# Streaming encoder step: three weight buffers in an empty operand region, and other pacing of operand building and of a reload

## The chip, the cores and the metric

The kernel runs on one core of one Trainium2 chip. A core has five engines with queues of their own: TensorE (matmul; PE in the rows, its weight loads PEld), VectorE (DVE), ScalarE (ACT), GpSimd (POOL) and SyncE (SP), which here issues the DMAs. Each engine runs its instructions in a fixed order, and an instruction that waits holds all behind it on its engine. The metric is the device time of one execution in microseconds (us), and lower is better. The kernel before took 1099.64 us (median of 3 runs, 1098.98 to 1100.81).

## The reference, cut to what matters

One step of a two-layer encoder over 1024 prompt rows and 64 rows of a running stream, 1088 in all. Layer 0 is a gated short convolution, layer 1 latent attention; everything that the edit touches lies in layer 0:

```python
def short_conv_mixer(h, conv_prev, w_in, conv_w, w_out):
    T = h.shape[1]
    b_gate, c_gate, xv, z = jnp.split(h @ w_in, 4, axis=-1)
    u = c_gate * xv
    up = jnp.concatenate([conv_prev.astype(u.dtype), u], axis=1)
    conv = up[:, 0:T] * conv_w[0]
    for k in range(1, CONV_WIDTH):
        conv = conv + up[:, k:k + T] * conv_w[k]
    y = (jax.nn.silu(z) * b_gate * conv) @ w_out
    return y, up[:, -(CONV_WIDTH - 1):]
```

`h` is the RMS-normed input (1024 channels), `w_in` is 1024 x 4096, all in float32. In layer 1 follow projections, attention with 16 heads and an output product, and at the end a last norm.

## The kernel before

**Precision.** Each float32 operand is split into a high part (`whi`, `bhi`, `t1h`: a cast on ScalarE) and a low part (`wlo`, `blo`, `t1l`: original less high part, on GpSimd or VectorE), and a product is three matmuls: high x high, high x low, low x high. `load_w` (L273 to L297) does it for a block of weights of 128 x 1024: a DMA into `wraw` (three buffers), the cast (L288), the subtraction (L292). `whi` and `wlo` have two buffers each.

**Layer 0.** The 1088 columns are two halves of 544 (`sc` = 0, 1), each two pieces of 272 (`c`). The output channels are eight tiles of 128 (`ct`), with four parts each (b, c, x, z).

- *Plain tiles*, ct = 0, 1, 2 of the first half: `conv_mm` makes 24 matmuls for each part and piece, so 48 for a block of weights. For ct = 1 and 2 one block is loaded ahead (`ahead`, L868 to L874). PSUM banks 0 to 4 take the results in turn.
- *Pairs*: for the other tiles two parts are computed together by a Strassen-like scheme: seven products (`p1`, `p5`, `p3` of the pair before, `p6`, `p4` of the pair before, `p2`, `p7`) of twelve matmuls each, on sums of weights and sums of inputs. `prep` makes the weight sums: `unit` splits a whole block (ScalarE and GpSimd), the pieces `t1`, `t2`, `t4` come from VectorE and ScalarE (L674 to L687). There are 10 pairs of the first half, then 16 of the second.
- *Operands of the pairs*: `build(sc, k)`, k = 0 to 3, makes the sums of inputs. `build(0, k)` runs beside the plain tiles (VectorE and GpSimd), `build(1, k)` beside the pairs of the first half (all on GpSimd). `squares(k)` sums the squares for the second half's norm: a ScalarE square into PSUM bank 7, a VectorE addition, in turn.
- *Gates*: `conv_evac` and `conv_tail` take results out of PSUM; part z goes VectorE (L532), ScalarE (L533), GpSimd (L534), VectorE (L536).
- *Reload*: the gated result of the first half goes to memory (`y_scratch`) and is read back by `reload_y` (L506 to L514) for the output product, once the last pair of the first half is done.

**What sets the order.** `jobs` is a list of generators; `side()` advances the first by a step, after each product (seven in a pair) and twice after each piece of a plain tile. `issue_after` on the last low subtraction keeps a job's instructions behind it. A scheduler turns the program into one order for each engine. The empty operand region is `R1`: its first 8704 columns hold the inputs of the plain tiles (`HS`, `LS`), its last 2048 the last block of ct = 0, and the rest is unused until `build(1, ...)`.

Of the kernel before, what the change touches and what calls it, by code (L numbers as in the profile page):

```python
# [25 lines left out]
KD = D // P  # L26
# [15 lines left out]
def r32(ap):  # L42
    return ap.bitcast(F32)
# [166 lines left out]
def kernel(ctx, tc, xT, small, w1, w2, w3, w3r, wpair, wqr, wv, wkT, w4,  # L210
# [13 lines left out]
    def nm(s):  # L224
        cnt[0] += 1
        return f"{s}_{cnt[0]}"
# [9 lines left out]
    def gps(tag="g", size=1):  # L236
        (b0, b1), k = turns[tag]
        turns[tag][1] = (k + size) % (b1 - b0)
        return PS[:, b0 + k:b0 + k + size, :].rearrange("p b n -> p (b n)")
# [27 lines left out]
    def ordered(ins):  # L267
        if keep_order[0]:
            tc.keep_in_program_order(ins)
# [4 lines left out]
    def load_w(src, n, view=None, into=None, lo_engine=None, cuts=None, shared=False):  # L274
        raw = wp[0].tile([P, WN[0]], F32, tag="wraw", name=nm("wraw"), bufs=3)
        if into is None:
            hi = wp[0].tile([P, WN[0]], F32R, tag="whi", name=nm("whi"), bufs=WN[1])
            lo = wp[0].tile([P, WN[0]], F32R, tag="wlo", name=nm("wlo"), bufs=WN[1])
        else:
            hi, lo = into  # L280
        if cuts:
            def part(a, b):
                ordered(A.copy(out=hi[:, a:b], in_=raw[:, a:b]))
                ordered((lo_engine or G).tensor_sub(lo[:, a:b], raw[:, a:b], r32(hi[:, a:b])))
            return hi, lo, lambda a, b: SP.dma_start(out=raw[:, a:b], in_=src[:, a:b]), part
        dst = raw[:, :n] if view is None else view(raw[:, :n])
        SP.dma_start(out=dst, in_=src)
        ins = A.copy(out=hi[:, :n], in_=raw[:, :n])  # L288
        hi_on[0] = ins.ins
        ordered(ins)  # L290
        m = n // 2 if shared else n
        ins = (lo_engine or G).tensor_sub(lo[:, :m], raw[:, :m], r32(hi[:, :m]))  # L292
        lo_on[0] = ins.ins
        ordered(ins)
        if shared:
            V.tensor_sub(lo[:, m:n], raw[:, m:n], r32(hi[:, m:n]))
        return hi, lo  # L297
# [77 lines left out]
    SC = 2 * NS  # L375
    REG = 14 * 4 * NS
    pX = tc.alloc_tile_pool(name="pX", bufs=1, side="right")
    R1 = pX.tile([P, REG], F32R, name="R1")
# [30 lines left out]
    def yh(k, c0, c1):  # L409
        return YHV[:, k, c0:c1]  # L410
# [15 lines left out]
    def staged(k):  # L426

        o = (2 * (k % 2) + k // 4) * SC
        return (STG, ST2)[k % 4 // 2][:, o:o + SC]
# [35 lines left out]

    def conv_mm(c, W, lag=0, mid=None):

        cs = slice(c * NS, (c + 1) * NS)
        wh, wl = W
        ps = gps()[:, :NS]  # L470
# [35 lines left out]
    def reload_y():  # L506

        for k in range(KD):
            y = STG[:, (k % 4) * SC:(k % 4 + 1) * SC]
            SP.dma_start(out=y, in_=y_d[k][:, :SC])  # L510
            yield
            A.copy(out=yh(k, 0, SC), in_=y)
            G.tensor_sub(yl(k, 0, SC), y, r32(yh(k, 0, SC)))  # L513
            yield  # L514

    def conv_state(ct, sc, u):
        if sc == 0:
# [69 lines left out]
    def build_first(k):  # L587
        yield from build(0, k)
        yield
        for kk in (k, k + 4):  # L590
            SP.dma_start(out=staged(kk), in_=xT[kk][:, SC:])
        yield

    def squares(k):

        for kk in (k, k + 4):
            for c in range(2):
                q, t = staged(kk)[:, c * NS:(c + 1) * NS], PS[:, 7, :NS]
                s = rb[:, SC + c * NS:SC + (c + 1) * NS]
                if kk == 0:  # L600
                    A.activation(out=s, in_=q, func=AF.Square)
                else:
                    A.activation(out=t, in_=q, func=AF.Square)
                    V.tensor_add(s, s, t)
                if k == 3:
                    yield
            if k < 3:
                yield

    jobs = []  # L610
# [182 lines left out]
    PARTS = [1, 2, 3, 0]  # L793
    STD = 3
    pairs = [f for sc, cts in ((0, range(STD, KD)), (1, range(KD))) for ct in cts for f in conv_pairs(ct, sc)]
    split_psum(g=(0, 6), q=(6, 8))
    ahead = []
    for ct in range(STD):
        if ct == 0:
            u, z = new_u(ct, 0), new_z()  # L800
            W = {}
            keep_order[0] = True
            *w, dma, part = load_w(w1[ct][PARTS[0]], 1024, lo_engine=V, cuts=True)
            W[PARTS[0]] = w
            dma(0, 256)
            x_dma(0, 0)
            dma(256, 1024)
            for k in range(1, KD):
                x_dma(0, k)
            part(0, 256)  # L810
            x_split(0, 0)
            part(256, 640)
            x_split(0, 1)
            part(640, 1024)
            for k in range(2, KD):
                x_split(0, k)
            *w, dma, part = load_w(w1[ct][PARTS[1]], 1024, lo_engine=V, cuts=True)
            W[PARTS[1]] = w
            dma(0, 1024)
            part(0, 512)  # L820
            part(512, 1024)
            pe_order[0] = True
            held = {c: [] for c in range(2)}

            def first(c, pi, lag=0, mid=None):
                held[c].append(conv_mm(c, W[PARTS[pi]], lag, mid))

            def evac(c, *pis):
                for pi in pis:
                    conv_evac(0, u, z, PARTS[pi], c, held[c][pi])  # L830

            first(0, 0, 3)
            for i, part in enumerate((3, 0)):
                W[part] = load_w(w1[ct][part], 1024, lo_engine=V, into=[p1.tile([P, 1024], F32R, tag=x, name=nm(x), bufs=1) for x in ("bhi", "blo")] if part else
                                 [R1[:, REG - n:REG - n + 1024] for n in (2048, 1024)])
                for k in range(2 * i, 2 * i + 2):
                    x_square(0, k)
            first(0, 1, 6)
            for k in range(KD):
                x_dma(1, k)  # L840
            for k in range(4, KD):
                x_square(0, k)
            first(0, 2, KD)
            first(0, 3, KD)
            for k in range(KD):
                x_split(1, k)
            end = finish_x(0)
            first(1, 0)
            first(1, 1, 0, end)
            evac(0, 0, 1)  # L850
            for k in range(4):
                x_square(1, k)
            first(1, 2)
            for k in range(4, KD):
                x_square(1, k)
            evac(0, 2, 3)
            first(1, 3)
            end = finish_x(1)

            def rest(u=u):  # L860
                end()
                evac(1, 0, 1, 2, 3)
                conv_state(0, 0, u)

            keep_order[0] = False
            split_psum(g=(0, 5), q=(7, 8))
            turns["g"][1] = 2
            jobs.extend([build_first(0), build_first(1), squares(0), build_first(2), squares(1), build_first(3), squares(2)])  # L868
        else:
            for pi, part in enumerate(PARTS):  # L870
                W = ahead.pop() if ahead else load_w(w1[ct][part], 1024)
                if pi < 3 or ct + 1 < STD:
                    ahead.append(load_w(w1[ct + (pi == 3)][PARTS[(pi + 1) % 4]], 1024))
                    paced["lo"] = lo_on[0]  # L874
                for c in range(2):
                    ps = conv_mm(c, W, (KD, 0)[c])
                    if ct == 1 and pi == c == 0:
                        rest()
                    if pi == c == 0:
                        u, z = new_u(ct, 0), new_z()  # L880
                    conv_evac(ct, u, z, part, c, ps)
                    side(2)
                if ct == STD - 1:
                    with tc.issue_after(lo_on[0]), tc.issue_after(hi_on[0]):
                        step(0, (0, 1, 1, 4)[pi])
        if ct:
            conv_state(ct, 0, u)
# [6 lines left out]
    def second_half():  # L894
        todo = {}

        def at(t, f):
            todo.setdefault(t, []).append(f)

        def factors():  # L900
            todo[9] = [rstd([rb[:, SC:]], rb[:, SC:], D, SC)]

        at(3, factors)
        for k in range(4):
            steps = build(1, k)
            for t in (0, 5, 6, 12):
                at(11 + 12 * k + t, lambda steps=steps: next(steps, None))
        for t in range(64):
            for f in todo.get(t, []):
                f()  # L910
            yield

    jobs.extend([squares(3), second_half()])
    step(1)

    pairs[2 * (KD - STD)].whole = True
# [19 lines left out]
    for dt in range(KD):  # L936
# [5 lines left out]
        for c, (c0, c1) in enumerate(CHK):  # L942
            n = c1 - c0
# [203 lines left out]
    for c, (c0, c1) in enumerate(CHK):  # L1147
        n = c1 - c0
# [675 lines left out]
    for dt in range(KD):  # L1824
# [9 lines left out]
        for c0, c1 in GRP[0]:  # L1834
            n = c1 - c0
# [125 lines left out]
```

## Time and profile before

| | us |
|---|---|
| median of 3 runs | 1099.64 |
| the profiled execution | 1099.2 |
| its span | 1097.4 |
| TensorE busy | 1048.0 (95%) |
| VectorE busy | 754.0 (69%) |
| ScalarE busy | 638.3 (58%) |
| GpSimd busy | 532.1 (48%) |

In the profile the busy times say how full an engine is over the whole span; a stage is read from its own rows. ct = 0 ends at about 36 us, the plain tiles of ct = 1 and 2 at 93.9, the pairs at about 383; output product, projections and attention follow. In a row of an engine in order of time stand its start, its duration, line, operation, output <- input, count, and in brackets the idle time before it with what released it.

### The profile page before, as it was taken

To read this page: it belongs to the slowest core of one execution; us is meant where nothing else is said; L and a number is where in the kernel's file an instruction comes from. 1 tells how busy PE (TensorE), PEld (TensorE's weight loads), DVE (VectorE), ACT (ScalarE), POOL (GpSimd) and SP (SyncE) were. 2 spreads that over 40 slices of the span, in tenths; PEclk is the share of its full clock that TensorE was granted. 3 is DMA by queue.
4 is the path that set the end of the run, shared out by engine and by line. 5 is a ranking of instruction groups with operands and counts; after the bars stand their busy time and mean duration, and the time that the engine had idled before them with its cause. 6 is when DMAs were issued, how large, how long until landed. Compare 5 with 4: busy or idle time off the path is not lost.

```text
span 1097.4 us, 19670 instructions
## 1 busy us (share of the span) xinstructions
PE 1048.0 (95%) x7123; PEld 1003.3 (91%) x7123; DVE 754.0 (69%) x1523; ACT 638.3 (58%) x1388; POOL 532.1 (48%) x446
## 2 busy tenths in 40 slices
PE   9989998989999999999899999999999999989994
PEld 8979998989999999999798999899999999879983
DVE  6888666756666445555996432788888888896456
ACT  5446676666666533345522334877787778785352
POOL 0475698886576622113452322445555545563243
PEclk9999999999999999999998999999999999999997
DMA  7244232442323244422142114433422331334224
GB/s 236 69 129 147 88 124 92 134 153 84 116 79 114 82 151 140 133 99 80 53 139 104 34 50 115 104 80 87 109 57 66 88 90 47 103 120 150 89 85 155
DMA packets 58145, 114.55 MB, mean 104 GB/s; under 512 B 8080, under 2 KB 32400, under 8 KB 58048
## 3 DMA queue, kind: packets, MB, share of 16 engines
q1 hardware_dynamic: 57840, 112.97, 33.7%
q8 instruction: 56, 0.92, 0.4%
q14 instruction: 41, 0.34, 0.1%
q10 hardware_dynamic: 144, 0.26, 0.1%
q0 software_dynamic: 64, 0.07, 0.0%
HBM read 79.27 MB, written 16.31 MB: 87 GB/s over the span
## 4 chain that ended last, share of the span: by engine, by line
PE 69%; DVE 10%; POOL 5%; issue 5%; DMA 4%; ACT 4%; SPq 1%; POOLq 0%; DVEq 0%; ACTq 0%
PE PS L301 48%; PE PS L1487 16%; PE PS L1526 5%; DMA QB<-stg 3%; POOL wlo L1765 1%; DMA wraw<-in_w 1%; POOL wlo L292 1%; DVE PS L488 1%; ACT PH L1539 1%; DVE OL L1011 1%; ACT stg L1603 1%; POOL R L565 1%; SPq L1613 1%; DVE PL L1543 0%; POOL R L513 0%
## 5 line engine op out<-in xcount | busy, mean ns | idle before, releaser
L301 PE MATMUL PS<-R,whi 128*128 128x272 f32 (+2 forms) x1662 | 370.4, 313 | 15.4 <-ACT whi L288 4.4
L301 PEld LDWEIGHTS PS<-R,whi 128*128 128x128 f32 x1662 | 276.6, 191 | 20.1 <-ACT whi L288 5.1
L301 PE MATMUL PS<-R,wlo 128*128 128x272 f32 (+2 forms) x888 | 265.9, 311 | 1.2 <-POOL wlo L292 1.2
L292 POOL TENSOR_TENSOR wlo<-wraw,whi 128x1024 fp32r<-128x1024 f32 x36 | 88.7, 2465 | 185.5 <-ACT whi L288 179.6
L301 PEld LDWEIGHTS PS<-R,wlo 128*128 128x128 f32 x888 | 164.1, 190 | 2.4 <-POOL wlo L292 1.9
L1487 PE MATMUL PS<-KB,QB 96*128 96x512 f32 (+11 forms) x576 | 125.2, 355 | 1.1 <-DVE SZ L1031 0.6
L1521 POOL TENSOR_SCALAR Pt<-Pt,st 128x640 f32<-128x640 f32 (+3 forms) x64 | 61.4, 961 | 86.4 <-DVE st L1517 85.9
L1487 PEld LDWEIGHTS PS<-KB,QB 96*128 96x128 f32 (+1 forms) x576 | 94.4, 190 | 9.4 <-DVE PL L1543 1.1
L1504 DVE TENSOR_REDUCE st<-PS 128x1 f32<-128x1024 f32 (+7 forms) x128 | 94.7, 748 | 10.9 <-PE PS L1487 10.2
L1543 DVE TENSOR_TENSOR PL<-PS,PH 128x512 fp32r<-128x512 f32 (+3 forms) x192 | 98.7, 547 | 3.1 <-ACT PH L1539 1.8
L1539 ACT CAST PH<-PS 128x512 fp32r<-128x512 f32 (+3 forms) x192 | 85.4, 497 | 14.7 <-PE PS L1526 13.5
L1487 PE MATMUL PS<-PH,VB 128*128 128x256 f32 x320 | 76.5, 279 | 0.0
L637 POOL TENSOR_TENSOR wlo<-wraw,whi 128x1024 fp32r<-128x1024 f32 x26 | 62.5, 2404 | 27.1 <-ACT whi L636 24.2
L1487 PE MATMUL PS<-PL,VB 128*128 128x256 f32 x320 | 75.3, 282 | 0.2 <-DVE PL L1543 0.2
L1513 ACT ACTIVATE Pt<-PS,st 128x640 f32<-128x640 f32 (+3 forms) x64 | 62.1, 970 | 5.7 <-DVE st L1517 2.6
L301 PE MATMUL PS<-R,bhi 128*128 128x272 f32 x320 | 61.1, 289 | 2.6 <-DVE z L763 1.0
L1487 PEld LDWEIGHTS PS<-PH,VB 128*128 128x128 f32 x320 | 60.8, 190 | 1.3 <-DVE PL L1543 0.8
L1487 PEld LDWEIGHTS PS<-PL,VB 128*128 128x128 f32 x320 | 61.1, 191 | 0.7 <-DVE PL L1543 0.4
L288 ACT CAST whi<-wraw 128x1024 fp32r<-128x1024 f32 (+1 forms) x37 | 38.2, 1033 | 38.3 <-PE PS L301 20.6
L1526 PE MATMUL PS<-ident,Pt 128*128 128x128 f32 x416 | 55.4, 274 | 0.2 <-ACT Pt L1513 0.2
L301 PEld LDWEIGHTS PS<-R,bhi 128*128 128x128 f32 x320 | 49.6, 188 | 3.7 <-DVE z L763 1.2
L1568 POOL TENSOR_TENSOR SZ<-SZ,ot 64x256 f32<-64x256 f32 x64 | 47.0, 746 | 11.7 <-DVE ot L1563 9.4
(438 smaller groups left out, 2623.0 us busy)
## 6 DMA issues: line engine op xcount, KB each, us to landing
wraw<-in_w SPq DMA_DIRECT2D x83, 512.0 KB, 3.6
KB<-stg SPq DMA_DIRECT2D x32, 256.0 KB, 3.8
QB<-stg SPq DMA_DIRECT2D x32, 256.0 KB, 4.7
braw<-in_w SPq DMA_DIRECT2D x13, 512.0 KB, 4.4
QB<-qr_scratch SPq DMA_DIRECT2D x32, 128.0 KB, 3.1
x<-x_scratch SPq DMA_DIRECT2D x8, 416.0 KB, 3.2
xr<-in_xT SPq DMA_DIRECT2D x16, 192.0 KB, 2.4
x_scratch<-xr SPq DMA_DIRECT2D x16, 192.0 KB, 1.9
```

The costliest lines, as they stand in the source:

```text
L288: ins = A.copy(out=hi[:, :n], in_=raw[:, :n])
L292: ins = (lo_engine or G).tensor_sub(lo[:, :m], raw[:, :m], r32(hi[:, :m]))
L301: ins = PE.matmul(ps, lhsT, rhs, start=start, stop=stop, skip_group_check=more)
L637: ins = eng.tensor_sub(lo, src, r32(hi))
L1487: pin(PE.matmul(ps, lhsT, rhs, start=start, stop=stop))
L1504: pin(V.tensor_reduce(out=st[:, 0:1], in_=TL["S", h, i], axis=AX.XY, op=ALU.max, negate=True))
L1513: pin(A.activation(out=Pt, in_=TL.pop(("S", h, i)), func=AF.Exp, bias=st[:, 0:1], accum_out=st[:, 1:2]))
L1521: pin(G.tensor_scalar(Pt, Pt, st[:, 2:3], 1.0, op0=ALU.mult, op1=ALU.mult))
L1526: pin(PE.transpose(out=tp[:, j * P:(j + 1) * P], in_=TL["P", h, i][:, (j0 + j) * P:(j0 + j + 1) * P], identity=ident))
L1539: pin(A.copy(out=hi, in_=src))
L1543: pin(V.tensor_sub(lo, src, r32(hi)))
L1568: pin(G.tensor_mul(sz, sz, TL.pop(("ot", h, pr))[rows]))
```

## The change

Line numbers after it are higher by 1 from L512 and by 3 at the end.

- The blocks of ct = 1 and 2 no longer go to `whi` and `wlo` but to three buffers of 2 x 1024 columns in `R1`, from column 8704, and up to three are loaded ahead. The third buffer (columns 12800 to 14848) overlaps the last block of ct = 0, and it takes the first load. `wraw` keeps its three buffers.
- `squares(2)` goes from the jobs of the plain tiles to those of the pairs, ahead of `squares(3)`, so `second_half` begins two steps later.
- In `second_half` the second and third step of a `build(1, k)` come at 6 and 7 instead of 5 and 6 steps after its first.
- `reload_y` waits six steps instead of one after each of its eight blocks.

```diff
@@ reload_y
             A.copy(out=yh(k, 0, SC), in_=y)
             G.tensor_sub(yl(k, 0, SC), y, r32(yh(k, 0, SC)))
-            yield
+            for _ in range(6):
+                yield
@@ plain tiles
-    ahead = []
+    ahead, todo = [], [(t, p) for t in range(1, STD) for p in PARTS]
@@
-            jobs.extend([build_first(0), build_first(1), squares(0), build_first(2), squares(1), build_first(3), squares(2)])
+            jobs.extend([build_first(0), build_first(1), squares(0), build_first(2), squares(1), build_first(3)])
         else:
             for pi, part in enumerate(PARTS):
-                W = ahead.pop() if ahead else load_w(w1[ct][part], 1024)
-                if pi < 3 or ct + 1 < STD:
-                    ahead.append(load_w(w1[ct + (pi == 3)][PARTS[(pi + 1) % 4]], 1024))
+                while len(ahead) < 3 and todo:
+                    n, (t, p) = len(todo) % 3, todo.pop(0)
+                    o = 2 * KD * SC + n * 2048
+                    ahead.append(load_w(w1[t][p], 1024, into=[R1[:, o + i:o + i + 1024] for i in (0, 1024)]))
                     paced["lo"] = lo_on[0]
+                W = ahead.pop(0)
@@ second_half
-            for t in (0, 5, 6, 12):
+            for t in (0, 6, 7, 12):
@@
-    jobs.extend([squares(3), second_half()])
+    jobs.extend([squares(2), squares(3), second_half()])
```

Three places of the engines' orders. GpSimd at the entry to the pairs, before (`wlo_860` and `wlo_934` are the last two plain blocks, `blo_1001`, `wlo_1084` and `wlo_1110` belong to pairs 0 and 1, L565 builds operands, L534 is the gate):

```order
L292 TENSOR_TENSOR wlo_860<-wraw_858,whi_859 128x1024
L565 TENSOR_TENSOR R_104<-ST_107,R_104 128x2x272 x2
L292 TENSOR_TENSOR wlo_934<-wraw_932,whi_933 128x1024
L637 TENSOR_TENSOR blo_1001<-braw_928,bhi_1000 128x1024
L534 TENSOR_TENSOR z_819<-z_819,acc_100 128x272
L637 TENSOR_TENSOR wlo_1084<-wraw_929,whi_1083 128x1024
L534 TENSOR_TENSOR z_819<-z_819,acc_100 128x272
L637 TENSOR_TENSOR wlo_1110<-wraw_1088,whi_1109 128x1024
```

And now (`R_98<-wraw_850` is the last plain block):

```order
L292 TENSOR_TENSOR R_98<-wraw_850,R_98 128x1024
L566 TENSOR_TENSOR R_104<-ST_107,R_104 128x2x272
L638 TENSOR_TENSOR blo_977<-braw_918,bhi_976 128x1024
L638 TENSOR_TENSOR wlo_1060<-wraw_919,whi_1059 128x1024
L638 TENSOR_TENSOR wlo_1086<-wraw_1064,whi_1085 128x1024
L566 TENSOR_TENSOR R_104<-ST_107,R_104 128x2x272
L535 TENSOR_TENSOR z_811<-z_811,acc_100 128x272 x2
```

The last plain block is done one place earlier, and three blocks of the pairs stand ahead of the last operand piece and of both gates.

VectorE at the same place, before (L532 is the gate of the second last plain block, for its two pieces; L675 to L687 and L637 make the pairs' pieces):

```order
L565 TENSOR_TENSOR R_104<-ST_107,R_104 128x2x272
L530 TENSOR_TENSOR u_817<-PS,u_817 128x272
L604 TENSOR_TENSOR acc_100<-acc_100,PS 128x272
L488 SCALAR_TENSOR_TENSOR PS<-u_817,sm,PS 128x272
L675 TENSOR_TENSOR wraw_929<-wraw_929,PS 128x512
L532 TENSOR_TENSOR z_819<-PS,acc_100 128x272
L488 SCALAR_TENSOR_TENSOR PS<-u_817,sm,PS 128x272
L676 TENSOR_TENSOR PS<-PS,braw_928 128x512
L637 TENSOR_TENSOR t1l_1070<-PS,t1h_1069 128x512
L532 TENSOR_TENSOR z_819<-PS,acc_100 128x272
```

And now, up to the same second gate (L580 to L583 make the last operand's sums):

```order
L566 TENSOR_TENSOR R_104<-ST_107,R_104 128x2x272
L638 TENSOR_TENSOR t1l_1046<-PS,t1h_1045 128x512
L680 TENSOR_TENSOR PS<-wraw_919,PS 128x512
L533 TENSOR_TENSOR z_811<-PS,acc_100 128x272
L638 TENSOR_TENSOR t2l_1051<-PS,t2h_1050 128x512
L688 TENSOR_TENSOR PS<-braw_918,PS 128x512
L676 TENSOR_TENSOR wraw_1065<-wraw_1065,PS 128x512
L677 TENSOR_TENSOR PS<-PS,wraw_1064 128x512
L533 TENSOR_TENSOR z_811<-PS,acc_100 128x272
```

More of the pairs' pieces stand ahead of the second gate, and the two L676/L677 of pair 0, which stood behind L565, are now among the sums ahead of L566.

GpSimd in the reload, before, from one `t4l` to the next (L513 is a reload block, L504 the second half's result):

```order
L637 TENSOR_TENSOR t4l_2564<-t_250_2561,t4h_2563 128x512
L637 TENSOR_TENSOR wlo_2725<-wraw_2622,whi_2724 128x1024
L513 TENSOR_TENSOR R_104<-STG,R_104 128x544 x2
L637 TENSOR_TENSOR wlo_2783<-wraw_2760,whi_2782 128x1024
L513 TENSOR_TENSOR R_104<-STG,R_104 128x544
L504 TENSOR_TENSOR R_104<-y_2826,R_104 128x272
L513 TENSOR_TENSOR YLB<-STG,R_104 128x544
L637 TENSOR_TENSOR t4l_2704<-t_267_2701,t4h_2703 128x512
```

And now:

```order
L638 TENSOR_TENSOR t4l_2682<-t_251_2679,t4h_2681 128x512
L638 TENSOR_TENSOR blo_2852<-wraw_2738,bhi_2851 128x1024
L513 TENSOR_TENSOR R_104<-STG,R_104 128x544
L504 TENSOR_TENSOR R_104<-y_2847,R_104 128x272
L638 TENSOR_TENSOR wlo_2905<-braw_2886,whi_2904 128x1024
L638 TENSOR_TENSOR t4l_2824<-t_270_2821,t4h_2823 128x512
```

One reload block stands between two `t4l` instead of four. In SyncE's queue the load of the fifth reload block stood ahead of a pair's second block of weights and now stands behind it.

## Rows read from the trace of the kernel before

**Rows 1.** Chain of waits, plain tiles: start us, us, what.
```profile
45.16 2.56 DVE R L576
...
89.79 4.84 DMA wraw<-in_w
```

**Rows 2.** TensorE's waits, 60 to 94 us: line, for whom, total us, times, longest.
```profile
PE PS L301 <- ACT whi L288: 4.4, 3, 2.8
PE PS L301 <- POOL wlo L292: 1.2, 3, 0.5
```

**Rows 3.** TensorE in order of time, plain tiles and entry to the pairs.
```profile
36.28 2.25 PE L301 MATMUL PS<-R,whi 128*128 128x272 f32 x16
...
49.49 2.16 PE L301 MATMUL PS<-R,whi 128*128 128x272 f32 x16
...
55.48 2.16 PE L301 MATMUL PS<-R,whi 128*128 128x272 f32 x16
...
64.43 3.48 PE L301 MATMUL PS<-R,whi 128*128 128x272 f32 x16 [2.81 <-ACT whi L288]
...
93.91 0.41 PE L301 MATMUL PS<-R,bhi 128*128 128x272 f32 x2
...
98.55 0.52 PE L301 MATMUL PS<-R,t2h 128*128 128x272 f32 x2 [1.47 <-ACT p L707]
```

**Rows 4.** VectorE in order of time, 37 to 93 us.
```profile
37.94 0.16 DVE L331 TENSOR_TENSOR rst<-rsy 128x3 f32<-128x3 f32 x1
...
45.07 2.65 DVE L576 TENSOR_TENSOR R<-STG,R 128x272 fp32r<-128x272 f32 x1
...
82.89 0.44 DVE L579 TENSOR_TENSOR ST<-ST 128x272 f32<-128x272 f32 x1 [2.16 <-POOL R L565]
...
92.45 0.43 DVE L532 TENSOR_TENSOR z<-PS,acc 128x272 f32<-128x272 f32 x1
```

**Rows 5.** GpSimd in order of time, plain tiles and reload.
```profile
45.03 2.40 POOL L292 TENSOR_TENSOR wlo<-wraw,whi 128x1024 fp32r<-128x1024 f32 x1 [1.45 <-ACT whi L288]
...
61.22 2.46 POOL L534 TENSOR_TENSOR z<-z,acc 128x272 f32<-128x272 f32 x1 [2.24 <-ACT z L533]
...
81.50 1.36 POOL L565 TENSOR_TENSOR R<-ST,R 128x544 fp32r<-128x544 f32 x1
...
232.36 2.68 POOL L513 TENSOR_TENSOR R<-STG,R 128x544 fp32r<-128x544 f32 x2
```

**Rows 6.** ScalarE in order of time, plain tiles and a build.
```profile
34.59 0.47 ACT L486 ACTIVATE PS<-u,sm 128x272 f32<-128x272 f32 x1
...
86.20 1.03 ACT L288 CAST whi<-wraw 128x1024 fp32r<-128x1024 f32 x1
...
166.25 0.42 ACT L575 CAST R<-ST 128x272 fp32r<-128x272 f32 x1 [4.25 <-POOL ST L573]
```

**Rows 7.** TensorE in order of time, builds of the second half and reload.
```profile
170.87 0.52 PE L301 MATMUL PS<-R,whi 128*128 128x272 f32 x2 [1.87 <-ACT p L707]
...
172.93 0.52 PE L301 MATMUL PS<-R,whi 128*128 128x272 f32 x2 [0.28 <-DVE z L771]
...
176.88 0.52 PE L301 MATMUL PS<-R,whi 128*128 128x272 f32 x2 [0.68 <-DVE u L763]
...
227.27 0.51 PE L301 MATMUL PS<-R,whi 128*128 128x272 f32 x2 [0.62 <-ACT p L707]
...
244.78 0.52 PE L301 MATMUL PS<-R,whi 128*128 128x272 f32 x2 [1.78 <-DVE u L763]
...
246.04 0.66 PE L301 MATMUL PS<-R,whi 128*128 128x272 f32 x2
...
249.42 0.42 PE L301 MATMUL PS<-R,t4h 128*128 128x272 f32 x2
```

**Rows 8.** VectorE in order of time, reload.
```profile
242.06 0.69 DVE L684 TENSOR_TENSOR t<-wraw,PS 128x512 f32<-128x512 f32 x1 [2.38 <-POOL t4l L637]
```

**Rows 9.** Busy time of GpSimd in a stretch: us, busy us, count, TensorE's clock, DMA share, GB/s.
```profile
230.00:242.00 12.00, 12.00 (x9) 1.00 0.38 126
```

## The prediction

> **What bounds the kernel now.** Read in this order: the busy rows of the page, the waits of TensorE in the plain stretch, the chain of waits there, then each engine's instructions in order of time. TensorE is busy 95% of the span, so only its idle stretches and its slow stretches can give time back. In the plain tiles of ct = 1 and 2 it waits 4.4 us for `whi` casts and 1.2 us for `wlo` subtractions [rows 2]; after the longest wait, 2.81 us, sixteen matmuls take 3.48 us instead of 2.16, another 1.3 us at the lower of the two clock levels [rows 3]. That is 6.9 us, and three weight buffers aim at it.
>
> The reader should see the other half in the chain of waits: from 45.16 us to the DMA that ends at 94.6 it holds pieces of VectorE, ScalarE, GpSimd and DMA and none of TensorE [rows 1]. TensorE's waits there are slack beside a longer chain: operand building, gates and squares, in fixed order on VectorE, ScalarE and GpSimd. So the first question is when that chain lets the first pair start, not when the weights are ready.
>
> Two more stretches belong to the edit. In the builds of the second half TensorE waits 1.87, 0.28 and 0.68 us, right after ScalarE sat 4.25 us in front of a cast that needs GpSimd's product [rows 6, 7]. In the reload it waits 0.62 and 1.78 us [rows 7], the latter behind VectorE, which waited 2.38 us for a late GpSimd subtraction [rows 8]; the stretch after it is slow: five triples of matmuls from 246.04 to 249.42 take 3.38 us [rows 7], where the normal pace is 48 in 5.99 us (49.49 to 55.48 [rows 3]), 0.374 for a triple and 1.50 for a product of twelve, so 1.5 us are lost.
>
> **The weights' buffers.** The order shows the eight casts at the same places in ScalarE's row, each now one load ahead. Casts 4 to 8 wait for TensorE to have left the buffer three tiles back, which it has. The first load goes to the third buffer, which overlaps the last weights of ct = 0; its cast stands behind ScalarE's gate product that ends at 35.06 [rows 6], when TensorE is past most of them, so the cast (1.03 us [rows 6]) ends at 36.1 and TensorE, free at 36.28 [rows 3], does not wait. The subtraction behind it (2.40 us [rows 5]) runs to 38.6, when the sixteen `hi` matmuls are just done. It costs something else: it lies beside the root chain of 128x3 products that begins at 37.94 [rows 4]. The nearest row of two such instructions is a VectorE subtraction of 272 columns with both inputs in SBUF, which took 2.65 us beside a `wlo` subtraction begun at 45.03 and ended when that ended, against 0.44 alone [rows 4, 5]. So the price is between 0 and 0.6 (37.94 to 38.6); I take 0.6, since the row shows full blocking.
>
> The Trainium skill (SBUF — State Buffer, Who interferes with whom) says that VectorE instructions with two SBUF inputs and GpSimd instructions that read SBUF exclude each other whatever their size, and that the one issued first holds the port to its end. By that rule the term is 0.6, without it 0; the 2.65 us row agrees, while the product of 2.46 us at 61.22 [rows 5] shows GpSimd losing to several VectorE instructions in a row.
>
> From there a plain tile takes 5.99 us. Eight tiles end near 87.2, with some 1.1 us of waiting left at tile 7, whose cast stands late in ScalarE's order; before, the last ended at 93.9. TensorE gains 6.7 us here, if anything can follow.
>
> **The entry to the pairs.** The first product of pair 0 needs PSUM bank 0, which the second gate evacuation of tile 7 frees (L532 before, L533 now). Before, that ran from 92.45 to 92.88, 1.0 us ahead of the product at 93.91 [rows 3, 4], so it cost nothing. Now TensorE arrives at 87.2 and it decides. The order rows show what VectorE does first: the four sums of the last operand, eight pieces of the pairs' operands, two conv products. And GpSimd has `blo` and two `wlo` subtractions, 2.4 us each, ahead of the last operand and of the gates, where it had one of the plain weights and then gaps.
>
> Up to 82.86 both orders are alike: GpSimd's subtraction of 81.50 ends and VectorE's L579 (now L580) starts at 82.89 [rows 4, 5]. Before, GpSimd had nothing ready then. Now `blo_977` is ready (its cast no longer waits behind squares), so it runs from 82.86 to 85.26, and by the 2.65 us row the VectorE sum then ends at 85.55 instead of 83.25: 2.3 us. L676, L531, L581 and L677 (0.69 us for a wide one [rows 8], 0.44 for a narrow one [rows 4], each overlapping the next by 0.1) bring VectorE to 87.45; the cast of the next `wlo` starts when L676 is done, 1.03 us [rows 6], so that GpSimd starts at 87.4. One of L582 and L583 meets it and waits: 1.9 us. L566 meets the third one: 1.55. Some 0.6 of these lies beside casts that the chain awaits anyway. Unblocked, the same list ends at 92.8, no sooner than before; with the three blocks at 98.05, with the 0.6 of above at 98.65. A fourth meeting (L582 as well) would make it 100.5, one less 97.4.
>
> So the first product starts at 98.65. Two products later (1.50 us each) is 101.65, and after some 11 us of idling I add one slow stretch, 1.3 us as at 64.43 [rows 3] (bounds 0 and 2.5). The third product, at 98.55 before [rows 3], stands at 102.95: **4.4 us lost** (bounds: 0.8 gained with no block, 6.5 lost with four). The casts and subtractions hoisted there are then done, so I expect no more waits in pairs 0 and 1.
>
> **Squares moved.** squares(2), four ScalarE and four VectorE instructions, leaves the crowded stretch and goes beside pairs 0 and 1, where TensorE has 21 us of work. The norm's matmuls stand two products later too, so I cost it at nothing; without that cover it is some 0.9 us for each of four (a narrow VectorE row of 0.44 and a narrow ScalarE row of 0.42 [rows 4, 6]).
>
> **Steps of the second half.** The cast that ScalarE stood 4.25 us in front of comes one product later (1.5 us), and in the new order two GpSimd subtractions with their casts pass between the product and that cast, so ScalarE no longer holds the gates behind it. I take all of 1.87 + 0.28 + 0.68 = **2.8 us gained** (bounds: 1.0 lost, if the later end of the builds makes pair 10 wait for as much as the 0.62 of [rows 7] or a little more, and 2.8). The end of the builds comes two steps later and should have room: pair 10 needs the last operand in its second product.
>
> **Reload.** Up to the `t4l` subtraction that ended at 242.06 GpSimd was busy for 12.0 of 12 us [rows 9], where a pair's seven products take TensorE 10.5: it is the slower of the two there. The order has four reload subtractions between that `t4l` and the one before it, 1.34 us each (two took 2.68 [rows 5]). In the new order one stands there, which takes 4.0 off: 8.0, well under 10.5. The 1.78 and the slow stretch of 1.5 go; the reload's DMA now stands behind the weights' in SP's queue, so the 0.62 goes too: **3.9 us gained** (bounds 1.8 and 4.4). The rest of the reload spreads over seven pairs, 1.4 us of GpSimd in each, which brings GpSimd to 9.4 at most where it had 8.0. After the pairs every engine's order is the same as before.
>
> **Sum.** 1099.2 (the profiled execution, span 1097.4 and 1.8 around it) + 4.4 - 2.8 - 3.9 = 1096.9. The median of the runs is 0.4 above that execution, so **1097.3**.
>
> **Rivals.** *The blocking does not add up* (17%): VectorE gets in between GpSimd's subtractions, as at 61.22. The first product then starts at 93.45, the third at 97.75, 0.8 gained; with the other two terms 7.5: 1092.1. For it: the one row of 2.46; against it: the 2.65.
> *The waits were the bound* (4%): everything that TensorE waited is recovered, the third product at 90.2, 8.3 gained: 1084.6. Against it stands the chain without TensorE.
> *Slower* (24%): the same blocking, once more. Four meetings put the first product at 100.5, and the clock stays low for 2 us of loss: 6.5 lost; and the builds gain nothing because GpSimd, late there, now only holds up a later cast. With 3.3 of the reload 3.2 us are lost: 1102.8. With the builds' gain the point from which it decides is a first product after 101.0.
> *It does not do what it says* is the forecast's own first half: the buffers remove the waits and no time.
>
> **How the numbers follow.** Forecast 55%, its own range 1094 to 1101. A change of 0.2%, 2.2 us, is about what a measurement of this kernel can tell from none. Of the forecast's 55 parts 26 lie more than 2.2 below 1099.64, 25 within, 4 above; the first two rivals are faster (21), of the slower one 20 parts lie above, 4 within. So faster 0.47, same 0.29, slower 0.24. The range runs from 1091 to 1103: it holds most of the first rival and most of the slower one.
>
> **What would show it.** Right: no wait of TensorE for `whi` in the plain tiles; the first product of pair 0 waiting some 11 us for VectorE's gate (98 to 101 us), with VectorE sums of over 2 us beside GpSimd subtractions from 82.9 on; the first reduced clock after that and none near 246; no ScalarE wait of 4 us for the builds; GpSimd with gaps in the reload. Wrong: a first product before 94 us, VectorE's sums at 0.44 throughout, or new waits in pairs 10 to 17.

## The result: 12 us slower, and the profile after

The changed kernel takes 1111.63 us (median of 4 runs), the kernel before 1099.80: a ratio of 1.0111 [1.0077, 1.0145]. The forecast was 1097.3, so the sign is wrong too. The profiled execution after takes 1111.65 us, its span is 1109.9.

TensorE in order of time, from ct = 0 to the entry of the pairs (answers [rows 2, 3]):

```profile
30.27 1.21 PE L301 MATMUL PS<-ident,rsy 128*128 128x128 f32 x6 [2.69 <-DVE rsy L333]
...
44.68 0.93 PE L301 MATMUL PS<-ident,rsy 128*128 128x128 f32 x6 [0.74 <-DVE rsy L333]
...
91.48 4.79 PE L301 MATMUL PS<-R 128*128 128x272 f32 x24 [2.53 <-DVE u L531]
...
103.65 0.79 PE L301 MATMUL PS<-R,bhi 128*128 128x272 f32 x2 [7.38 <-DVE z L533]
...
109.22 0.43 PE L301 MATMUL PS<-R,t2h 128*128 128x272 f32 x2
```

The waits for `whi` in the plain tiles are gone but for 0.39 us at 78.95 us and 0.46 us for a subtraction at 81.68, as forecast (some 1.1 left). In their place stand waits for VectorE: 2.69 us already in ct = 0, where there was none, 2.53 in the last plain tile, 7.38 in front of the first product of pair 0. The third product (109.22) is 10.7 us later than in [rows 3], not 4.4. After the first of these waits the granted clock was 0.59 from 30 to 34 us: from 30.27 to the sums of the second root (40.08) pass 9.81 us, where the same stretch takes 8.41 in run 3 below.

VectorE (answers [rows 4]), then GpSimd (answers [rows 5]), then ScalarE (answers [rows 6]):

```profile
24.11 2.32 DVE L331 TENSOR_TENSOR rst<-rsy 128x3 f32<-128x3 f32 x1
26.47 2.29 DVE L332 SCALAR_TENSOR_TENSOR rst<-rst,rsv 128x3 f32<-128x3 f32 x1
...
41.04 1.62 DVE L328 TENSOR_SCALAR rst<-rsv 128x3 int32<-128x3 int32 x1
...
87.89 2.59 DVE L580 TENSOR_TENSOR ST<-ST 128x272 f32<-128x272 f32 x1 [3.06 <-POOL R L566]
...
92.30 2.60 DVE L582 TENSOR_TENSOR ST<-ST 128x272 f32<-128x272 f32 x1
...
95.23 2.19 DVE L583 TENSOR_TENSOR ST<-ST 128x272 f32<-128x272 f32 x1
...
103.07 0.43 DVE L533 TENSOR_TENSOR z<-PS,acc 128x272 f32<-128x272 f32 x1
```

```profile
24.01 4.73 POOL L292 TENSOR_TENSOR R<-wraw,R 128x1024 fp32r<-128x1024 f32 x2 [22.70 <-ACT R L288]
...
40.25 2.38 POOL L292 TENSOR_TENSOR R<-wraw,R 128x1024 fp32r<-128x1024 f32 x1 [1.34 <-PE PS L301]
...
86.49 1.36 POOL L566 TENSOR_TENSOR R<-ST,R 128x544 fp32r<-128x544 f32 x1
87.81 2.37 POOL L638 TENSOR_TENSOR blo<-braw,bhi 128x1024 fp32r<-128x1024 f32 x1
92.23 4.89 POOL L638 TENSOR_TENSOR wlo<-wraw,whi 128x1024 fp32r<-128x1024 f32 x2 [2.06 <-ACT whi L637]
```

```profile
22.89 1.99 ACT L288 CAST R<-wraw 128x1024 fp32r<-128x1024 f32 x2
...
211.27 0.65 ACT L565 CAST R<-ST 128x544 fp32r<-128x544 f32 x1 [4.18 <-POOL ST L582]
```

Read the first two fences side by side. Each long VectorE instruction begins while a GpSimd subtraction runs and ends when that ends or up to 0.3 us later; the same 128x3 operation takes 0.16 us in [rows 4]. At 24 us two subtractions in a row catch two root instructions in a row. They can run then because the casts of the second and third load find empty buffers at 22.89 us. Before, the first two casts of the plain blocks stood so, and the first subtraction behind them so:

```profile
25.19 1.05 ACT L288 CAST whi<-wraw 128x1024 fp32r<-128x1024 f32 x1 [2.64 <-issue]
...
28.82 1.05 ACT L288 CAST whi<-wraw 128x1024 fp32r<-128x1024 f32 x1
```

```profile
26.33 2.39 POOL L292 TENSOR_TENSOR wlo<-wraw,whi 128x1024 fp32r<-128x1024 f32 x1 [25.01 <-ACT whi L288]
```

The first idled 2.64 us at the same place of ScalarE's order; the row names no releaser, by the program it is TensorE leaving `whi`. The second stood behind four other ScalarE instructions (L346, L444 and two L447), which it now precedes. At 88 us it is the chain that the forecast described.

Further on, the builds and the reload (answers [rows 7]), and the stretch of the reload as a whole:

```profile
183.30 0.39 PE L301 MATMUL PS<-R,wlo 128*128 128x272 f32 x1 [0.88 <-POOL wlo L638]
...
215.71 0.52 PE L301 MATMUL PS<-R,whi 128*128 128x272 f32 x2 [1.72 <-ACT p L708]
...
254.42 0.52 PE L301 MATMUL PS<-R,whi 128*128 128x272 f32 x2 [0.53 <-DVE u L764]
```

```profile
215.00:260.00 45.00, 42.86 (x332) 41.94 (x333) 29.55 (x61) 27.50 (x58) 32.82 (x19) 1.00 0.37 119
```

The long ScalarE wait of the builds was not removed: 4.25 us at 166.25 [rows 6] became 4.18 us at 211.27, and TensorE's wait behind it moved with it. The 1.78 us of the reload and the reduced clock behind them are gone (granted clock 1.00 from 215 to 260 us), and small waits of some 0.5 us take their place.

**Where the 12.5 us of span arise.** ScalarE copies 78 products `p` out of PSUM, three in each pair; they serve as milestones. The first and last start of the copies stand in the view of that line, before and after:

```profile
L707 ACT COPY p<-PS x78: 367/385/401, 98.1 to 380.7; 128x272 f32<-128x272 f32 x78
```

```profile
L708 ACT COPY p<-PS x78: 363/386/400, 106.7 to 392.0; 128x272 f32<-128x272 f32 x78
```

In between, the first copy of pair 1 is 10.6 us late (115.52 for 104.93), the last of pair 9 12.5 (219.47 for 207.00), the last of all 11.4. So: 10.6 up to the entry (0.85 of it a later start of this execution), 1.9 for the builds, -1.1 for the reload, 1.1 behind the pairs, where no order changed. The last two are smaller than the difference between two executions of one kernel (last rows of the table below).

### The profile page after: what moved, and what is told of

Read it like the earlier page. It is cut to its first block, busy times and chain, and to the rows that moved or that the text cites. A ratio compares the mean times of both kernels' runs of the same rounds, so it can differ in the third digit from the quotient of the medians.

```text
span 1109.9 us, 19659 instructions
## 1 busy us (share of the span) xinstructions
PE 1053.3 (95%) x7123; PEld 1007.3 (91%) x7123; DVE 767.7 (69%) x1523; ACT 637.4 (57%) x1388; POOL 532.9 (48%) x446
## 4 chain that ended last, share of the span: by engine, by line
PE 64%; DVE 13%; POOL 6%; issue 5%; DMA 5%; ACT 5%; SPq 1%; POOLq 0%; ACTq 0%; DVEq 0%
PE PS L301 43%; PE PS L1490 16%; PE PS L1529 5%; DMA QB<-stg 3%; DMA wraw<-in_w 2%; POOL wlo L1768 1%; DVE PS L488 1%; ACT PH L1542 1%; POOL blo L638 1%; DVE OL L1014 1%; POOL R L566 1%; ACT stg L1606 1%; POOL t4l L638 1%; DVE qt L1215 1%; SPq L1616 1%
## 5 line engine op out<-in xcount | busy, mean ns | idle before, releaser
L301 PE MATMUL PS<-R,whi 128*128 128x272 f32 (+2 forms) x1406 | 327.7, 316 | 10.5 <-DVE SZ L1034 5.0
L301 PEld LDWEIGHTS PS<-R,whi 128*128 128x128 f32 x1406 | 239.0, 190 | 15.4 <-issue 4.4
L301 PE MATMUL PS<-R,wlo 128*128 128x272 f32 (+2 forms) x760 | 238.1, 315 | 0.9 <-POOL wlo L638 0.9
L301 PEld LDWEIGHTS PS<-R,wlo 128*128 128x128 f32 x760 | 143.9, 190 | 1.3 <-POOL wlo L638 1.1
L292 POOL TENSOR_TENSOR wlo<-wraw,whi 128x1024 fp32r<-128x1024 f32 x28 | 68.4, 2444 | 155.0 <-ACT whi L288 151.9
L638 POOL TENSOR_TENSOR wlo<-wraw,whi 128x1024 fp32r<-128x1024 f32 x26 | 62.6, 2409 | 21.7 <-ACT whi L637 21.3
L301 PE MATMUL PS<-R 128*128 128x272 f32 x432 | 57.1, 293 | 3.4 <-DVE u L531 2.5
L301 PEld LDWEIGHTS PS<-R,bhi 128*128 128x128 f32 x320 | 50.7, 192 | 10.6 <-issue 7.6
L301 PEld LDWEIGHTS PS<-R 128*128 128x128 f32 x432 | 55.9, 193 | 4.0 <-DVE u L531 2.8
```

The source lines that it names most:

```text
L301: ins = PE.matmul(ps, lhsT, rhs, start=start, stop=stop, skip_group_check=more)
L638: ins = eng.tensor_sub(lo, src, r32(hi))
```

## The experiments

Each ratio is to the kernel before, timed on the same chip (the runs below used three), with its 95% interval, from five rounds or, for the changed kernel, from four runs. A is the time from the first copy to the last of pair 9 (entry's end and builds), B from there to the last copy (reload), C from there to the end. All four times are read from one profile each.

| kernel | ratio | first copy | A | B | C |
|---|---|---|---|---|---|
| before | 1 | 98.1 | 108.9 | 173.7 | 716.7 |
| after | 1.0111 [1.0077, 1.0145] | 106.7 | 112.7 | 172.6 | 717.8 |
| buffers alone | 1.0057 [1.0042, 1.0073] | 103.5 | 110.6 | 173.8 | 716.6 |
| the other three edits | 1.0040 [1.0024, 1.0056] | 97.6 | 111.6 | 176.0 | 715.4 |
| after, root held free | 1.0087 [1.0063, 1.0112] | 101.8 | 111.8 | 175.4 | 715.1 |
| after, entry put back | 1.0089 [1.0069, 1.0110] | 104.1 | 112.6 | 175.0 | 719.4 |
| after, both | 1.0053 [1.0034, 1.0072] | 101.6 | 112.5 | 174.0 | 716.6 |
| steps alone | 1.0022 [1.0006, 1.0038] | 98.7 | 110.8 | 173.8 | 717.7 |
| reload alone | 1.0015 [1.0000, 1.0030] | 98.9 | 108.9 | 176.1 | 716.4 |
| squares(2) alone | 1.0049 [1.0032, 1.0065] | 98.1 | 112.4 | 172.1 | 719.9 |
| second half two products later | 1.0029 [1.0013, 1.0046] | 99.0 | 111.2 | 173.8 | 719.0 |
| less work for GpSimd | 0.9994 [0.9976, 1.0013] | 98.6 | 108.1 | 173.1 | 719.5 |
| before, again | one run, 1105.53 us | 97.5 | 108.9 | 176.4 | 721.0 |
| squares(2) alone, again | one run, 1104.60 us | 98.2 | 112.3 | 173.7 | 718.6 |

The last two rows say how to read the others: A repeats to 0.1 us, the first copy to 0.7, B and C differ by 2.7 and 4.2 us between two executions of the same kernel. Differences in A are evidence from one profile; of B and C only the ratios over many runs are.

**1. Buffers alone.**
```diff
-                W = ahead.pop() if ahead else load_w(w1[ct][part], 1024)
...
+                while len(ahead) < 3 and todo:
...
+                W = ahead.pop(0)
```


> The kernel before with the three weight buffers alone; squares, steps of the second half and reload as before. Theory T (the buffers let casts and subtractions run early, GpSimd's subtractions then hold up VectorE's chain, at the first root chain near 24 us and again at the last operand sums near 88 us): nearly the whole loss is here, 1108 to 1113 us, with two 128x3 VectorE instructions of over 2 us near 24 to 28 us and a wait of 5 us or more ahead of the first product of pair 0. Rival R (the loss comes from the other three edits, the pacing above all): 1097 to 1102 us.


```profile
23.87 2.32 DVE L331 TENSOR_TENSOR rst<-rsy 128x3 f32<-128x3 f32 x1
26.22 2.26 DVE L332 SCALAR_TENSOR_TENSOR rst<-rst,rsv 128x3 f32<-128x3 f32 x1
```
1106.26 us, 6.3 slower by the ratio: half of the loss, between the two theories. In ct = 0 the root instructions take 2.32 and 2.26 us and TensorE waits 3.75, as in the changed kernel. At the entry one sum of four is caught (2.58 us; squares(2) still stands between the sums there), and the first product waits 4.28 us.

**2. The other three edits.**
```diff
-                while len(ahead) < 3 and todo:
...
-                W = ahead.pop(0)
+                W = ahead.pop() if ahead else load_w(w1[ct][part], 1024)
...
```


> The changed kernel with the weight buffers undone: squares(2) later, the steps of the second half and the reload paced anew. T: no loss up to the third product of pair 0 (98 to 99 us, as before), and the builds and the reload give back 1 to 6 us: 1094 to 1099 us. Rival R: the loss is here, 1106 to 1112 us, as new waits of TensorE in the pairs.


1103.55 us, 4.4 slower by the ratio: neither theory. The loss is shared, and the gains that were forecast for these edits do not exist. So each got a run of its own (5, 6, 7).

**3. The root held free.** One GpSimd product of 0.2 us reads the first root's result, and the subtractions of the second and third load (`behind`) follow it.
```diff
             end = finish_x(0)
+            gate_on = G.tensor_mul(gate, root_on[0], root_on[0]).ins
...
+            if behind is not None:
+                stack.enter_context(tc.issue_after(behind))
             ins = (lo_engine or G).tensor_sub(lo[:, :m], raw[:, :m], r32(hi[:, :m]))
```


> The changed kernel with one more GpSimd instruction, a 128x3 product that reads the result of the first root chain and stands ahead of the first two weight subtractions; every other instruction keeps its place. T: the two 128x3 VectorE instructions fall from 2.3 us to below 0.3, TensorE's 2.7 us wait near 30 us goes, and the first product of pair 0 starts 3.5 to 5 us earlier, at 98.5 to 100.2 us: 1105 to 1109 us. Rival Q (the early stall is swallowed by later waits, the entry alone decides): first product still at 102 to 104 us and 1110 to 1113 us.


VectorE, GpSimd and TensorE in order of time:
```profile
23.51 0.16 DVE L334 TENSOR_TENSOR rst<-rsy 128x3 f32<-128x3 f32 x1
23.70 0.16 DVE L335 SCALAR_TENSOR_TENSOR rst<-rst,rsv 128x3 f32<-128x3 f32 x1
...
27.73 0.44 DVE L466 TENSOR_TENSOR rb2kp<-acc 128x272 f32<-128x272 f32 x1 [2.50 <-ACT acc L350]
```
```profile
25.32 0.20 POOL L854 TENSOR_TENSOR gate<-rsy 128x3 f32<-128x3 f32 x1 [24.00 <-DVE rsy L336]
25.48 4.95 POOL L295 TENSOR_TENSOR R<-wraw,R 128x1024 fp32r<-128x1024 f32 x2
```
```profile
86.54 3.28 PE L304 MATMUL PS<-R 128*128 128x272 f32 x24 [2.56 <-DVE u L535]
98.71 0.79 PE L304 MATMUL PS<-R,bhi 128*128 128x272 f32 x2 [8.90 <-DVE z L537]
```
The first root runs at 0.16 us again (the second root's int32 shift still takes 0.98 us at 36.71), TensorE's 2.69 us wait is gone, and the first product starts at 98.71; the forecast had said 98.65. That is 4.9 us earlier than after, 1.0 of it from an earlier start of the execution (the first root's sums at 21.26 us, after 22.25, before 21.40). By pair 9 the profile is 5.8 us ahead of the changed kernel. The median, 1109.36, lies just above T's range and shows only 2.3 of it, with intervals that overlap; B took 2.8 back in the profiled execution, as much as B differs between two executions (2.7).

**4. The entry put back.** The two subtractions of pair 0's operands stand behind those of the last operand.
```diff
+    for t, src in kept:
+        with tc.issue_after(low_on[0]):
+            paced["lo"] = low_on[0] = G.tensor_sub(t[1], src, r32(t[0])).ins
```


> The changed kernel with the two 128x1024 subtractions of pair 0's operands put behind the subtractions of the last operand in GpSimd's order (the third, of pair 1, follows them). T: the operand sums of VectorE fall from 2.2 to 2.6 us to 0.4, the second gate evacuation ends 4 to 6 us earlier and the first product of pair 0 starts at 98 to 100 us: 1105 to 1109 us. Rival Q' (GpSimd itself is the bound, its three subtractions only come later): TensorE then waits for blo or wlo, first product, or the ones after it, no earlier than before, 1110 to 1114 us.


```profile
88.93 0.44 DVE L580 TENSOR_TENSOR ST<-ST 128x272 f32<-128x272 f32 x1 [3.09 <-POOL R L566]
...
91.19 0.43 DVE L582 TENSOR_TENSOR ST<-ST 128x272 f32<-128x272 f32 x1
...
102.67 0.44 DVE L537 TENSOR_TENSOR z<-PS,z 128x272 f32<-128x272 f32 x1 [3.28 <-POOL z L535]
```
```profile
98.94 0.79 PE L301 MATMUL PS<-R,bhi 128*128 128x272 f32 x2 [5.30 <-DVE z L533]
```
All sums take 0.43 or 0.44 us. From the end of GpSimd's last early subtraction to the first product there are 10.05 us (88.89 to 98.94), where the changed kernel and run 3 have 15.8 each: the three blocks cost 5.75. Half is given back: the gate's GpSimd product now stands behind the three subtractions (VectorE waits 3.28 us for it), and at the last copy of pair 0 only 2.9 of the 5.75 are left. 1108.95 us, as theory T said, with part of its rival in it.

**5. Both.** 


> The changed kernel with both repairs: the 128x3 GpSimd product ahead of the first two weight subtractions, and the two operand subtractions of pair 0 behind those of the last operand. Theory T (two collisions that add): no VectorE sum or root instruction of over 1 us beside a GpSimd subtraction, first product of pair 0 at 92.5 to 95 us, third product at 97.5 to 101 us: the loss that is left is that of the three other edits, 1102 to 1106 us. Rival Q (with the first repaired, the second costs nothing or the reverse, another engine bounds the entry): first product at 96 us or later, 1107 to 1110 us.


1105.46 us, in T's range; the first product at 96.45 is 1.5 us later than T allowed. No operand sum and nothing of the first root is caught. But the second root's int32 shift is, beside the first load's subtraction (38.85 to 41.23), which T had excluded, and so is another instruction: the square of the norm's factors, beside the second of the two subtractions that begin at 25.48 as in run 3.
```profile
28.09 2.40 DVE L466 TENSOR_TENSOR rb2kp<-acc 128x272 f32<-128x272 f32 x1 [2.85 <-ACT acc L350]
...
39.63 1.62 DVE L331 TENSOR_SCALAR rst<-rsv 128x3 int32<-128x3 int32 x1
```
The square came 0.36 us later than in run 3: there 0.08 us before the second subtraction began (27.81), here 0.27 us after (27.82). There it took 0.44 us, here 2.40. Why it came later was not settled. The two repairs add up within the intervals (1.0111 to 1.0053), and what is left is about the other three edits (1.0040).

**6. Steps alone.**
```diff
-            for t in (0, 5, 6, 12):
+            for t in (0, 6, 7, 12):
```


> The kernel before with the second half's steps at 0, 6, 7, 12 alone. Theory S (ScalarE's wait for GpSimd's sums is moved, not removed): the 4.25 us wait near 166 us goes, one of about 4 us comes at the last operand near 200 us; pairs 4 to 8 run 1 to 2 us earlier, pair 10 some 1 to 2 us later than before: 1100 to 1103 us. Rival U (the step gains, as forecast, and the loss of the three edits together sits elsewhere): 1096 to 1099 us, TensorE's waits between 160 and 220 us falling by 2 us or more.


```profile
179.57 0.65 ACT L564 CAST R<-ST 128x544 fp32r<-128x544 f32 x1 [4.15 <-POOL ST L581]
```
```profile
184.12 0.52 PE L301 MATMUL PS<-R,bhi 128*128 128x272 f32 x2 [1.78 <-ACT p L707]
```
1101.36 us, as S said, A 1.9 longer. The 4.25 us wait left the third operand's first step [rows 6] and came back at its last step as 4.15 (S had expected it at the last operand), with TensorE's wait behind it.

**7. squares(2) alone, and the second half two products later.**
```diff
-build_first(3), squares(2)])
+build_first(3)])
...
-    jobs.extend([squares(3), second_half()])
+    jobs.extend([squares(2), squares(3), second_half()])
```
```diff
-    jobs.extend([squares(3), second_half()])
+    jobs.extend([squares(3), iter((1, 1)), second_half()])
```


> The kernel before with squares(2) behind the plain tiles alone. Theory S: its eight instructions fall into pairs 0 and 1, where VectorE is full, and cost up to 1.3 us: 1099.5 to 1101.5 us. Rival U: nothing: 1098.5 to 1100 us.

> The kernel before with the second half begun two products later by two empty steps; squares(2) stays in the plain tiles. Theory S (what squares(2) costs is that it pushes the second half two products on): as with squares(2) moved, the long ScalarE wait moves to the operand near 191 us, 1101 to 1104.5 us. Rival W (its eight instructions beside pairs 0 and 1 cost): 1099 to 1100.5 us and pairs 0 and 1 as before.


```profile
191.09 0.42 ACT L575 CAST R<-ST 128x272 fp32r<-128x272 f32 x1 [4.27 <-POOL ST L573]
```
```profile
190.84 0.42 ACT L575 CAST R<-ST 128x272 fp32r<-128x272 f32 x1 [4.26 <-POOL ST L573]
```
1104.28 us, above both of its theories, and 1102.57 us, as its S said. The two empty steps alone make A 2.4 us longer, squares(2) moved 3.5; both put the long ScalarE wait into the fourth operand. So two thirds of what squares(2) costs in A is that `jobs` is one queue and everything behind it starts two products later. The other 1.1 us fit pairs 0 and 1, where the first copy of pair 1 comes 1.8 us late with squares(2) moved and on time with the empty steps.

Both runs, and every kernel with squares(2) moved, also have a collision that the forecast did not look for, in the root of the second half's norm: its int32 shift (L328, 128x5) takes 0.17 us at 106.63 in the kernel before, 1.98 at 110.43 in the first of these runs, 2.04 at 110.19 in the second and 2.04 at 119.91 in the changed kernel. It costs little: TensorE's wait for the norm's factors goes from 0.68 us to 0.93 in the first run and 0.95 in the second.

**8. Reload alone.**
```diff
-            yield
+            for _ in range(6):
+                yield
```


> The kernel before with six yields in the reload alone. Theory S (the reload's ScalarE copies and GpSimd subtractions cost a little in each pair that holds one): the 1.78 us wait near 245 us and the slow clock behind it go, 2 to 3 us gained by pair 13, and seven or eight waits of 0.3 to 0.8 us in pairs 13 to 23 give back 2 to 4.5: 1099 to 1103 us. Rival U: the waits in pairs 13 to 23 belong to the shifted phase of the other edits, the gain stays: 1096 to 1098 us.


```profile
265.88 0.52 PE L301 MATMUL PS<-R,whi 128*128 128x272 f32 x2 [0.55 <-DVE u L764]
...
283.60 0.52 PE L301 MATMUL PS<-R,bhi 128*128 128x272 f32 x2 [0.67 <-ACT p L708]
```
1100.73 us: no gain, at most 3.3 us lost. In the profile the big wait goes and small ones come, about as S said: five of 0.53 to 0.91 us behind 260 us, where the first profile of the kernel before has none and its second one two (0.34 and 0.52). Over the profiles of the table B is 174.8 us on average with the new reload (six) and 173.8 with the old one (eight), where 3.9 less had been forecast.

**9. Less work for GpSimd.**
```diff
-        E, F = (G, G) if sc else (V, G)
+        E, F = (G, V) if sc else (V, G)
```


> The kernel before with two of the second half's GpSimd subtractions per operand (128x544 each, eight in all) on VectorE; every time offset as before. Theory S (GpSimd is late there, ScalarE's wait of some 4 us for its sums stands in whichever operand the order happens to put it, and only less work for GpSimd removes it): no ScalarE wait of over 2 us for GpSimd between 130 and 215 us, TensorE's 2.8 us near 171 to 177 go: 1096 to 1098.5 us. Rival V (VectorE then waits beside GpSimd's subtractions, as at the entry of the changed kernel): VectorE instructions of over 1.5 us in the builds, new waits of TensorE, 1099.5 to 1104 us.


```profile
167.12 0.42 ACT L575 CAST R<-ST 128x272 fp32r<-128x272 f32 x1 [3.02 <-POOL ST L573]
```
```profile
147.31 2.23 DVE L565 TENSOR_TENSOR R<-STG,R 128x544 fp32r<-128x544 f32 x1 [0.84 <-ACT R L564]
```
1099.03 us, no change. Both theories are half right: ScalarE's wait shrinks to 3.02 us, TensorE's 2.8 us behind it to 1.6, and A by 0.8; and six of VectorE's eight new subtractions are caught beside GpSimd (1.35 to 2.23 us, where the same form takes 0.7 in the entry), with new waits of TensorE of 0.82 and 1.10 us near 150 us.

**10. Two kernels once more.**


> The kernel before once more, for a second profile. If the spread of some 3 us between runs comes from the later stages, whose order no edit touches: the pairs end within 1 us of the first profile, relative to the first product, and the slow stretches of TensorE's clock behind 500 us lie elsewhere or are more or fewer.

> The kernel with squares(2) moved alone, for a second profile. If its 3 us behind 600 us (slow clock at 691 us) belong to the run: gone or elsewhere, with the pairs' end 1.5 to 2.2 us later than before; if they belong to the edit: again a slow stretch near 690 us.


Busy times and, third from the right, granted clock of 685 to 700 us: before, squares(2) alone, before again, squares(2) again.
```profile
685.00:700.00 15.00, 13.91 (x89) 12.12 (x87) 10.71 (x26) 11.97 (x30) 5.04 (x8) 1.00 0.51 117
```
```profile
685.00:700.00 15.00, 13.41 (x66) 11.97 (x65) 6.76 (x14) 8.68 (x17) 4.31 (x7) 0.77 0.68 152
```
```profile
685.00:700.00 15.00, 13.76 (x69) 12.34 (x68) 7.18 (x16) 9.17 (x19) 4.61 (x8) 0.77 0.60 144
```
```profile
685.00:700.00 15.00, 13.88 (x88) 12.45 (x88) 8.20 (x20) 10.69 (x22) 4.64 (x8) 1.00 0.66 154
```
The slow clock there belongs to the execution, not to the edit: each kernel shows it once. But the expectation that the pairs end alike failed: the unchanged kernel's B is 2.7 us longer the second time.

## Why the prediction was wrong, step by step

- **Plain tiles: right.** The waits for casts went, and TensorE arrived early at a chain that decides.
- **The root chain, 0.6 us (bounds 0 and 0.6): this step failed.** It priced the first load's subtraction, which comes last, against the second root, and took the other seven casts as "at the same places in ScalarE's row". For the two that matter this was wrong: one kept its place and lost the wait in front of it, the other moved ahead of four instructions. Their subtractions came onto the first root chain (the first at 24.01, before at 26.33). Run 3 puts a price on it: with those two behind the root, GpSimd's last operand piece ahead of the entry ends at 82.91 us instead of 87.85, some 4 earlier beyond the earlier start. The third product then stands at 103.39, 4.8 us later than before, where 4.4 had been forecast; without, 10.7, or 9.8 less the later start. The meeting that was priced took 0.8 us (0.98 for 0.17 in run 3), above its bound, but did not reach the entry: the next weight subtraction begins at 45.01, before at 45.03.
- **The entry: right in mechanism, 0.6 us too small.** Three sums are blocked (2.59, 2.60, 2.19), the third of them L583 where L566 had been forecast. From the end of GpSimd's operand piece to the first product there are 15.8 us, 10.05 with the blocks gone (run 4); the forecast's own working has 15.2 (82.86 to 98.05) and 9.9 (to 92.8). That run 3's first product came within 0.1 us of the forecast's 98.65 is partly luck: 0.6 too little here, and 0.6 of the root that did not arrive. The slow stretch, sized at 1.3 (bounds 0 and 2.5), took 1.7 in run 3 and 2.6 in the changed kernel (98.71 to 103.39 and 103.65 to 109.22, less two products of 1.50; granted clock 0.64 from 98 to 104 us and 0.50 from 103 to 109).
- **squares(2) at nothing: failed.** The cover (TensorE's work in pairs 0 and 1) hid its instructions but for 1.8 us at pair 1, of which 1.1 is left in A; that it delays the second half, and with it the norm's root into a subtraction, was not looked at. 3.5 us in A.
- **Steps, 2.8 gained: failed.** "ScalarE no longer holds the gates" was read from the third operand alone. The wait of some 4.2 us stands at 166 us before, at 180 with the steps alone, at 191 with squares(2) moved or the second half shifted, at 201 with the three edits, at 211 after; it never went. This also fits that the three edits, 0.22, 0.15 and 0.49% slower alone, are 0.40% slower together: a wait that each of them moves is paid once. That it is one and the same wait was not tested further.
- **Reload, 3.9 gained: failed in size.** The 1.78 and the slow stretch went; small waits spread over the pairs after it cost about as much. That they come from the reload's cast and subtraction in each pair is likely but was not shown.
- The rival "slower" named the right cause, more meetings, and put them in the wrong place, as a fourth at the entry instead of two in ct = 0. Its other half, that the builds gain nothing because GpSimd now holds up a later cast, is what run 6 shows. Its 6.5 us do not follow from its own terms: 100.5, two products of 1.50 and 2 us of clock, less 98.55, are 7.0.

The Trainium skill (SBUF — State Buffer, Who interferes with whom) says that the order of issue, not an instruction's shape, decides which of VectorE and GpSimd waits. The runs agree: 0.36 us earlier or later made 0.44 or 2.40 us of the same instruction (runs 3 and 5), and where VectorE came first, GpSimd's subtraction took 2.61 us instead of 2.37.

## What to carry to other kernels

A buffer that is freed earlier moves not one instruction but all that its old wait held back: list every instruction that may now start, with its engine, and look what the other of VectorE and GpSimd does at that time. Where a long wait sits in front of an engine that is late for the whole stage, a new offset moves the wait to the next operand; look for it in all operands before counting it as gained. Before sizing anything below 3 us, profile the unchanged kernel twice and trust only the stretches that repeat.

## What the runs showed of the hardware that was not expected

- The smallest VectorE instructions pay the full price: 128x3 ones that take 0.16 us took 2.32 and 2.29 beside two GpSimd subtractions in a row, each waiting for one of them.
- An instruction with a single input in SBUF waits as well: the int32 shift of 128x3 at 41.04 took 1.62 us, 0.17 alone, and in run 4 both int32 operations of the first root did (2.10 and 2.31 us). The operation just ahead of the shift, which reads PSUM, took 0.16 us beside the same subtraction (40.84). The Trainium skill (SBUF — State Buffer, Who interferes with whom) lists the shift's operation, `tensor_scalar`, among those that can use both ports and so contend with GpSimd; the trace agrees.
- After the wait of 2.53 us at 91.48, 24 matmuls took 4.79 us (granted clock 0.69 from 91 to 96.5 us, so part of it at the lower level); after one of 2.56 us in run 3, the same 24 took 3.28 (1.00 from 86 to 90). A wait of one length was followed by a slow stretch in one execution and not in the other.
